# Gate rows, B, first scan tiles, layer norm steps and last tile of a conv and state-space layer moved in the order of work

## The chip, the cores and the metric

The kernel runs on one core of one Trainium2 chip. That core has TensorE (PE) for matrix products, VectorE (DVE), ScalarE (ACT) and GpSimd (POOL) for elementwise work, and SyncE (SP), whose queue issues nearly all DMA transfers. Each engine takes its own instructions strictly in order, and waits where the data or the buffer of the next one is not there yet. The metric is the time of one launch on the device, in microseconds; the median of the runs counts.

## The reference

One layer over 2048 tokens of width 1024, with a context of 256 tokens: a normed and modulated input, one projection to five parts of 1024 columns, a gated depthwise convolution of 31 taps on a 32 x 64 grid with a layer norm behind it, a state-space recurrence in both directions over 64 groups, an output projection with a gate, and a last norm.

```python
h = rmsnorm(x, norm_g) * (1 + scale) + shift
p = split(h @ w_in)                       # value, glu gate, silu gate, u, silu gate of y
# conv branch
v = p[0] * sigmoid(p[1])
v = dwconv_latent(v, conv_dw, conv_db)    # 31 taps: rows of the grid for half the channels, columns for the rest
v = silu(layernorm(v, conv_ln_g, conv_ln_b)) * silu(p[2])
# state-space branch: lam_bar, b_bar from a, log_dt, b; the context gives the first state
hf = scan(u, lam_bar_f, b_bar_f); hb = scan(u, lam_bar_b, b_bar_b, reverse)
y = gelu(real(hf . c_f) + real(hb . c_b) + d * u)
y = y * sigmoid(y @ glu_w + glu_b) * silu(p[4])
mix = concat(v, y) @ w_out
out = rmsnorm(x + gate * mix, final_g)
...
```

## The kernel before

Every large product is split in three: an operand a becomes hi + lo, and hi x hi, lo x hi and hi x lo are summed (lines 129, 134 and 135). `project` makes one 128 x 512 tile of a projection from eight row tiles, that is from 24 such matmuls. `whi` (ACT, line 243) and `wlo` (POOL, line 244) split a weight tile that was loaded as `wraw` (or `wuc`, for the context's columns).

The work goes through five stages, told apart by the line that is busy.

The **head**, to some 163 us, loads x in four blocks of 512 tokens (`xt`), norms and modulates them, and computes the context projections (`psc`, `usc`, stored as `uc_d`) and the first channel tile of the convolution. `gate_rows` adds the output gate's rows into one PSUM tile `gps`; four ACT copies `gr` (line 717) write them to `gate_d`.

The **conv stage**, to some 699 us, takes one channel tile of 128 after the other. PE computes its glu gate and value (`glu`, line 299, writes `v`), and DVE applies the taps of the tile before (`taps`, line 300 on): three accumulators fP, fQ and fR, of which fP and fR lie in PSUM and are begun by ACT (lines 319 and 323) and fQ lies in SBUF; each tap is one DVE instruction of line 336. `beside`, called once behind each projection, emits RATE = 4.8 taps and the glu that is held back, and then takes one step of the generator `toeplitz`. That makes, for four groups at a time, the factors `ff` (POOL products ff and pp, lines 387 and 388, four DVE sums, line 396), the discretised B `bb` (`bbar`, every fourth time), the product `tz` on PE (line 407) and its copy `tzs` to the store `toe_d`. The steps of the generator stand in the code behind the taps of each call, so on DVE the four sums stand behind those taps. The value products go to the pool `mm` with three PSUM banks. At the end, `gate_tiles` begins the projections of the silu gate (`gs`, stored as `cg_d`).

The **scan stage**, to some 1232 us, works in 32 blocks of two groups. `load` fetches U (the inputs), F, M and, for every second block, B. `inputs` builds KB from B and X from KB on POOL (lines 835 to 851), turns X on PE (`et`, line 855), and ACT copies that to E; then come the chunk states S on PE (line 894), the recurrence on DVE and the readout. The tiles B, KB, kt, X, xp, E, ys and the four tt belong to pools of this stage, which open when the conv stage's are closed. The projections of the remaining gate tiles run between them.

The **GLU stage**, to 1417 us, has 32 products of y with `glu_w`. A table `aside` hangs other work behind product n of them; the eight steps of the layer norm of the first 512 tokens (the generator `layer_norm(0)`) are hung behind the products (6, 10, 14, 15, 17, 18, 20, 21). The steps are: loads lx and their sum lsum (POOL); mean mu on PE and squares; variance va and its root, which DVE makes into a diagonal dg; rb, the diagonal spread over a tile on PE, and the multiplies; then four pairs of multiplies by lg, each pair with its own load and stores to `mix_d`.

The **out projection**, from 1417 us on, has sixteen row tiles t_ of four products each. The layer norm of the next 512 tokens runs in four steps behind the products of LN_QUARTER in four row tiles; all four pairs of lg are in the last step and share one buffer. `mix_in` loads `mr` from `mix_d`, and `split_mix` splits it into mh (ACT) and ml (DVE). `finish` norms a row tile and stores it (line 1287).

## Time and profile before

| | us |
|---|---|
| median of three runs (lowest, highest) | 1800.89 (1800.38, 1803.52) |
| the profiled execution, its own time | 1801.97 |
| its span in the profile | 1800.2 |
| PE busy | 1725.8 (96%) |
| weight loads on PE, beside the matmuls | 1354.6 (75%) |
| DVE, ACT, POOL busy | 1410.8 (78%), 584.9 (32%), 561.5 (31%) |

A row of the profile names an engine, a line of the kernel, an operation with its output and inputs (`tz<-ff,bb` is tile tz from ff and bb, buffer numbers left out), how many there were, and in square brackets the idle time of the engine ahead of it with what ended that idle time. PE is busy nearly all the time, so the few places where it is not are what the views are searched for. A busy PE is not PE at its peak: the granted clock says at which of its two levels it ran.

### The profile page before, as it was taken

Reading aid. Unit: us, or ns where it says so; the run is one execution under the profiler, and the core shown is the slowest. Engines: PE = TensorE matmul, PEld = TensorE weight load, DVE = VectorE, ACT = ScalarE, POOL = GpSimd, SP = SyncE. Lnnn points to the kernel's source line nnn. Section 1 sums busy time; section 2 is a strip of 40 time slices with the busy share of each in tenths; the row PEclk is TensorE's granted clock in tenths of the full one; section 3 lists DMA queues with packets and bytes.
Section 4 is the critical chain, followed back from the end, with each engine's and each line's share of the span. In section 5 each row is a group of like instructions: output and inputs, shape, how many; then the busy total and the mean of one; then the engine's idle time right before and its main releaser. Section 6 shows DMA issues by size and latency. Waiting matters only on the chain.

```text
span 1800.2 us, 23670 instructions
## 1 busy us (share of the span) xinstructions
PE 1725.8 (96%) x8728; PEld 1354.6 (75%) x8728; DVE 1410.8 (78%) x2063; ACT 584.9 (32%) x904; POOL 561.5 (31%) x550
## 2 busy tenths in 40 slices
PE   7999799999999998999999999999989989999998
PEld 2675577787788886777777777778778768887887
DVE  7863799999998987999999999995665755656533
ACT  4542211221222113343433433354453422222211
POOL 0632243344432113665554655320210041212000
PEclk9999899999999998999999999999999999999999
DMA  9604131222222123243333333363738837363621
GB/s 342 231 18 127 34 104 44 96 79 68 97 98 76 50 76 109 88 121 106 101 117 115 98 122 105 105 225 120 215 113 279 303 108 206 118 198 122 176 97 44
DMA packets 175724, 227.45 MB, mean 126 GB/s; under 512 B 38516, under 2 KB 117492, under 8 KB 174584
## 3 DMA queue, kind: packets, MB, share of 16 engines
q1 hardware_dynamic: 175608, 225.94, 39.0%
q8 instruction: 69, 1.13, 0.3%
q14 instruction: 47, 0.39, 0.1%
HBM read 147.36 MB, written 78.52 MB: 125 GB/s over the span
## 4 chain that ended last, share of the span: by engine, by line
PE 65%; DVE 20%; DMA 6%; issue 3%; ACT 2%; POOL 2%; SPq 1%; DVEq 0%; ACTq 0%; POOLq 0%
PE ps L129 13%; PE ps L134 13%; PE ps L135 13%; PE pso L135 4%; PE pso L134 4%; PE pso L129 4%; DVE fQ L336 4%; PE S L894 3%; DVE fR L336 3%; PE Y L945 3%; DVE fP L336 3%; DMA mix_d<-lx 2%; PE Y L936 1%; DVE lo L223 1%; PE adps L620 1%
## 5 line engine op out<-in xcount | busy, mean ns | idle before, releaser
L129 PE MATMUL ps<-hi,whi 128*128 128x512 f32 x1248 | 499.1, 400 | 1.2 <-ACT v L296 1.2
L134 PE MATMUL ps<-lo,whi 128*128 128x512 f32 x1248 | 492.7, 395 | 0.0
L135 PE MATMUL ps<-hi,wlo 128*128 128x512 f32 x1248 | 491.6, 394 | 0.3 <-POOL wlo L244 0.3
L129 PEld LDWEIGHTS ps<-hi,whi 128*128 128x128 f32 x1248 | 235.9, 189 | 62.1 <-issue 9.3
L135 PEld LDWEIGHTS ps<-hi,wlo 128*128 128x128 f32 x1248 | 236.1, 189 | 55.5 <-issue 3.5
L134 PEld LDWEIGHTS ps<-lo,whi 128*128 128x128 f32 x1248 | 236.2, 189 | 53.4 <-issue 5.2
L129 PE MATMUL pso<-woh,mh 128*128 128x512 f32 (+1 forms) x528 | 206.2, 391 | 0.8 <-ACT woh L1026 0.4
L134 PE MATMUL pso<-wol,mh 128*128 128x512 f32 (+1 forms) x528 | 203.8, 386 | 2.1 <-DVE wol L1029 2.1
L135 PE MATMUL pso<-woh,ml 128*128 128x512 f32 (+1 forms) x528 | 204.4, 387 | 0.7 <-DVE ml L1029 0.5
L244 POOL TENSOR_TENSOR wlo<-wraw,whi 128x1024 fp32r<-128x1024 f32 x37 | 97.3, 2630 | 174.2 <-ACT whi L243 174.2
L336 DVE SCALAR_TENSOR_TENSOR fQ<-v,sml,fQ 128x960 f32<-128x960 f32 (+11 forms) x120 | 149.2, 1243 | 0.0
L336 DVE SCALAR_TENSOR_TENSOR fP<-v,sml,fP 128x960 f32<-128x960 f32 (+10 forms) x112 | 121.0, 1080 | 24.7 <-ACT fP L319 24.7
L336 DVE SCALAR_TENSOR_TENSOR fR<-fS,comb,fR 128x960 f32<-128x960 f32 (+11 forms) x120 | 128.1, 1067 | 0.0
L918 DVE TENSOR_TENSOR_SCAN t<-mag,t 128x287 f32<-128x287 f32 x128 | 122.0, 1011 | 0.0
L134 PEld LDWEIGHTS pso<-wol,mh 128*128 128x128 f32 x528 | 99.8, 189 | 24.7 <-DVE wol L1029 3.1
L129 PEld LDWEIGHTS pso<-woh,mh 128*128 128x128 f32 x528 | 99.8, 189 | 22.9 <-ACT woh L1026 1.4
L135 PEld LDWEIGHTS pso<-woh,ml 128*128 128x128 f32 x528 | 99.7, 189 | 21.7 <-DVE ml L1029 1.5
L243 ACT ACTIVATE whi<-wraw 128x1024 fp32r<-128x1024 f32 x37 | 39.1, 1055 | 212.2 <-PE ps L134 172.9
L129 PE MATMUL ps<-yh,gwh 128*128 128x512 f32 x256 | 100.7, 393 | 0.0
L134 PE MATMUL ps<-yl,gwh 128*128 128x512 f32 x256 | 99.9, 390 | 0.0
L135 PE MATMUL ps<-yh,gwl 128*128 128x512 f32 x256 | 99.9, 390 | 0.0
L1064 POOL TENSOR_TENSOR lsum<-lx 128x512 f32<-128x512 f32 x4 | 5.5, 1362 | 301.7 <-DMA lx<-cv_d 301.7
(295 smaller groups left out, 2804.8 us busy)
## 6 DMA issues: line engine op xcount, KB each, us to landing
wraw<-in_w_in SPq DMA_DIRECT2D x37, 512.0 KB
mr<-mix_d SPq DMA_DIRECT2D x32, 512.0 KB
wa<-in_w_ada SPq DMA_DIRECT2D x32, 256.0 KB
xt<-in_x_t SPq DMA_DIRECT2D x32, 256.0 KB
u_d<-us SPq DMA_DIRECT2D x32, 256.0 KB
f_d<-ff SPq DMA_DIRECT2D x32, 256.0 KB
cv_d<-v SPq DMA_DIRECT2D x8, 1024.0 KB
cg_d<-gs SPq DMA_DIRECT2D x32, 256.0 KB
```

The lines of the kernel that those rows point to most:

```text
L129: i = nc.tensor.matmul(ps, wh, rh, start=first, stop=False)
L134: nc.tensor.matmul(ps, wh, rl, start=False, stop=False)
L135: last[0] = nc.tensor.matmul(ps, wl, rh, start=False, stop=end)
L223: st(lo, xts[k], sh_, hi.bitcast(F32), op0=ADD, op1=SUB)
L243: act(hi, raw, AF.Copy)
L244: pt(lo, raw, hi.bitcast(F32), op=SUB)
L336: yield st(at(acc, lo_ + o, hi_ + o), at(src, lo_ + j, hi_ + j), tap[n](j), at(acc, lo_ + o, hi_ + o), op0=MUL, op1=ADD)
L620: nc.tensor.matmul(adps[32 * c:32 * c + 32], sil[:, k], was[h, k, c], start=(k == 0), stop=(k == KT - 1), skip_group_check=True)
L894: m = nc.tensor.matmul(Sf[h_, o + c0:o + c1], k.E[:, d, i, h_], seq[g][d][:, c0:c1], start=True, stop=True, skip_group_check=True)
L918: nc.vector.tensor_tensor_scan(dst[:, d, 0:L], mag8[:, g0 + d:g0 + d + 1].to_broadcast([P, L]), src[:, d, 0:L], 0.0, op0=MUL, op1=ADD)
L936: m = nc.tensor.matmul(Y[:, g], k.M[:, g], k.U[:, g, NX:NCOL], start=True, stop=False, skip_group_check=True)
L945: m = nc.tensor.matmul(Y[:, g], k.F[h_, i, d], hs, start=False, stop=(i == 1 and d == 1), skip_group_check=True)
```

## The change

The diff does six things.

The PSUM tile `gps` goes to a new pool `gpp` of one bank, which `tz` uses after it (the pool of tz is gone). The copies `gr` are put into a function `gate_out`, called at the first `beside`, and are ordered on ACT behind the fR of the first channel tile.

`bq`, the load of B for `bbar`, has a tile of its own and is issued with the load of cc, and `beside` steps the generator ahead of the taps, not behind them.

In the scan, B, KB, kt and xp lie in the pool `par`, which is open from the start; X and E take turns in the two buffers of `ff`; ys lies in `stage` and tt in a pool of its own.

The layer norm's steps hang behind the products (6, 10, 14, 16, 18, 19, 20, 21), and for the second norm LN_QUARTER is (0, 5, 8, 10).

In the last row tile, xt times fg is formed piece by piece as `gx` behind each product, and the last scaling is done for one half by ACT, with a store on ACT's own queue, and for the other by DVE.

```diff
-LN_QUARTER = (0, 4, 7, 9)
+LN_QUARTER = ((), (0, 5, 8, 10), (0, 4, 7, 9), (0, 4, 7, 9))
...
+    tp = parstack.enter_context(tc.tile_pool(name="toe", bufs=1))
...
+    gpp = tstack2.enter_context(tc.tile_pool(name="gpp", bufs=1, space=PS))
...
-        act(r_, S_, AF.Identity, scale=tap[2](0), bias=db[:, 1, ct:ct + 1])
+        late.fr = act(r_, S_, AF.Identity, scale=tap[2](0), bias=db[:, 1, ct:ct + 1])
...
+    def b_load(q):
+        bq = late.fir.tile([P, 2, 16, GH], F32, tag="bq", name="bq")
+        for i, nm in enumerate(("b_re", "b_im")):
+            nc.sync.dma_start(bq[:, i], ins[nm][:, 16 * q:16 * q + 16, :])
+        return bq
+
+    def bbar(q, bq):
...
-        bq = stage.tile([P, 2, 16, GH], F32, tag="sa", name="bq")
-        for i, nm in enumerate(("b_re", "b_im")):
-            nc.sync.dma_start(bq[:, i], ins[nm][:, g_, :])
...
+            if b4 % 4 == 0:
+                bq = b_load(b4 // 4)
...
-            tz = late.tps.tile([P, 2, P], F32, tag="tz", name="tz")
+            tz = gpp.tile([P, 512], F32, tag="g", name="tz")[:, 0:2 * P].rearrange("p (d q) -> p d q", d=2)
...
-    gps = nps.tile([P, 512], F32, tag="gps", bufs=1, name="gps")
+    gps = gpp.tile([P, 512], F32, tag="g", name="gps")
...
-    for i in range(2):
-        for c in range(2):
-            gr = stage.tile([1, 512], F32, tag="sa", name="gr")
-            act(gr, gps[64 * i + 32 * c:64 * i + 32 * c + 1], AF.Copy)
-            nc.sync.dma_start(gate_d[i:i + 1, c * 512:(c + 1) * 512], gr)
+
+    def gate_out():
+        for i in range(2):
+            for c in range(2):
+                gr = stage.tile([1, 512], F32, tag="sa", name="gr")
+                g_ = act(gr, gps[64 * i + 32 * c:64 * i + 32 * c + 1], AF.Copy)
+
+                tc.add_manual_dep(g_.ins, late.fr.ins.name, mybir.DependencyInfo(
+                    mybir.DependencyClass.NoSync, mybir.DependencyReason.DATA), reason="order")
+                nc.sync.dma_start(gate_d[i:i + 1, c * 512:(c + 1) * 512], gr)
+
...
         def beside():
 
+            next(toe, None)
             due[0] += RATE
...
-            next(toe, None)
+            if late.fr is not None and not late.gated:
+                late.gated = True
+                gate_out()
...
-                B_ = [s1p.tile([P, 4, GH], F32, tag=f"B{i}", name=f"B{i}") for i in range(2)]
+                B_ = [par.tile([P, 4, GH], F32, tag=f"B{i}", name=f"B{i}") for i in range(2)]
...
-                KB = KBs[b // 2] = [s2p.tile([P, 4, GH], F32, tag=f"KB{i}", name=f"KB{i}") for i in range(2)]
-                kt = s1p.tile([P, 4, GH], F32, tag="kt", name="kt")
+                KB = KBs[b // 2] = [par.tile([P, 4, GH], F32, tag=f"KB{i}", bufs=2, name=f"KB{i}") for i in range(2)]
+                kt = par.tile([P, 4, GH], F32, tag="kt", name="kt")
...
-            X = [s1p.tile(shp, F32, tag=f"X{i}", name=f"X{i}") for i in range(2)]
-            xp = s1p.tile(shp, F32, tag="xp", name="xp")
+            X = tp.tile([P, 2, G, T, GH], F32, tag="ff", bufs=2, name="X")
+            X = [X[:, i] for i in range(2)]
+            xp = par.tile(shp, F32, tag="xp", name="xp")
...
-            k.E = s1p.tile([P, G, 2, P], F32, tag="E", name="E")
+            k.E = tp.tile([P, G, 2, P], F32, tag="ff", bufs=2, name="E")
...
-            tt = k.tt = [s1p.tile([P, G, NCOL], F32, tag=f"t{i}", name=f"t{i}") for i in range(4)]
+            tt = k.tt = [s0p.tile([P, G, NCOL], F32, tag=f"t{i}", name=f"t{i}") for i in range(4)]
...
-            ys = s1p.tile([P, G, NC_], F32, tag="ys", name="ys")
+            ys = stage.tile([P, G, NC_], F32, tag="sa", name="ys")
...
-    for n in (6, 10, 14, 15, 17, 18, 20, 21):
+    for n in (6, 10, 14, 16, 18, 19, 20, 21):
...
-            for cs_ in [slice(0, 1024)] if t_ < 15 else [slice(0, 512), slice(512, 1024)]:
-                st(xt[:, cs_], xt[:, cs_], rs, fg[:, cs_], op0=MUL, op1=MUL)
-                nc.sync.dma_start(ov[row(t_)[0], row(t_)[1], cs_], xt[:, cs_])
+            if t_ < 15:
+                st(xt, xt, rs, fg, op0=MUL, op1=MUL)
+                nc.sync.dma_start(ov[row(t_)[0], row(t_)[1], :], xt)
+                return
+
+            act(xt[:, 0:512], late.gx[:, 0:512], AF.Identity, scale=rs)
+            vs(xt[:, 512:1024], late.gx[:, 512:1024], rs, None, op0=MUL)
+            nc.scalar.dma_start(ov[row(t_)[0], row(t_)[1], 0:512], xt[:, 0:512])
+            nc.sync.dma_start(ov[row(t_)[0], row(t_)[1], 512:1024], xt[:, 512:1024])
...
-                        if t_ < 12 and 4 * (t_ % 4) + 2 * (1 - k8) + i in LN_QUARTER:
+                        if t_ < 12 and 4 * (t_ % 4) + 2 * (1 - k8) + i in LN_QUARTER[t_ // 4 + 1]:
...
+                    if i == 0:
+                        late.gx = wp.tile([P, 1024], F32, tag="wraw", bufs=1, name="gx")
+                    vt(late.gx[:, cols[i]], xt[:, cols[i]], fg[:, cols[i]], op=MUL)
```

On ACT, at the end of the head, this stands in a row before (whi splits a weight tile, v is the glu gate's sigmoid, us a tile of u):

```order
L320 ACTIVATE fQ<-v,sml 128x32x32
L243 ACTIVATE whi<-wraw 128x1024
L428 ACTIVATE us<-ps 128x2x256
L296 ACTIVATE v<-ps 128x512 x2
L717 ACTIVATE gr<-gps 1x512 x4
L319 ACTIVATE fP<-v,db,sml 128x1024
L323 ACTIVATE fR<-fS,db,comb 128x1024
```

and this after:

```order
L321 ACTIVATE fP<-v,db,sml 128x1024
L322 ACTIVATE fQ<-v,sml 128x32x32
L325 ACTIVATE fR<-fS,db,comb 128x1024
L245 ACTIVATE whi<-wraw 128x1024
L435 ACTIVATE us<-ps 128x2x256
L298 ACTIVATE v<-ps 128x512 x2
L726 ACTIVATE gr<-gps 1x512 x4
```

The beginnings fP and fR of the first channel tile moved ahead of the four copies gr, of a weight split and of two v.

On DVE, in the conv stage, around the second set of four sums ff, before:

```order
L336 SCALAR_TENSOR_TENSOR fR<-fS,comb,fR 128x32x27
L336 SCALAR_TENSOR_TENSOR fP<-v,sml,fP 128x32x27
L336 SCALAR_TENSOR_TENSOR fQ<-v,sml,fQ 128x32x28
L299 TENSOR_TENSOR v<-ps,v 128x512
L336 SCALAR_TENSOR_TENSOR fR<-fS,comb,fR 128x32x27
L336 SCALAR_TENSOR_TENSOR fP<-v,sml,fP 128x32x26
L336 SCALAR_TENSOR_TENSOR fQ<-v,sml,fQ 128x32x26
L396 TENSOR_TENSOR ff<-ff,pp 128x256 x4
```

and after:

```order
L338 SCALAR_TENSOR_TENSOR fR<-fS,comb,fR 128x32x27
L403 TENSOR_TENSOR ff<-ff,pp 128x256 x4
L338 SCALAR_TENSOR_TENSOR fP<-v,sml,fP 128x32x27
L338 SCALAR_TENSOR_TENSOR fQ<-v,sml,fQ 128x32x28
L301 TENSOR_TENSOR v<-ps,v 128x512
L338 SCALAR_TENSOR_TENSOR fR<-fS,comb,fR 128x32x27
L338 SCALAR_TENSOR_TENSOR fP<-v,sml,fP 128x32x26
L338 SCALAR_TENSOR_TENSOR fQ<-v,sml,fQ 128x32x26
```

The sums moved ahead of five taps and one glu.

On POOL, in the head, among the splits wlo of the context's weight tiles, before:

```order
L244 TENSOR_TENSOR wlo<-wuc,whi 128x1024 x8
L194 TENSOR_TENSOR sqa<-sqa,sq 128x512
L244 TENSOR_TENSOR wlo<-wuc,whi 128x1024
L194 TENSOR_TENSOR sqa<-sqa,sq 128x512
L244 TENSOR_TENSOR wlo<-wuc,whi 128x1024
```

and after:

```order
L246 TENSOR_TENSOR wlo<-wuc,whi 128x1024 x3
L853 TENSOR_TENSOR KB_5425<-B_5416,kbr 128x64
L856 TENSOR_TENSOR KB_5426<-B_5416,kbi 128x64
L854 TENSOR_TENSOR kt<-B_5417,kbi 128x64
L855 TENSOR_TENSOR KB_5425<-KB_5425,kt 128x64
L857 TENSOR_TENSOR kt<-B_5417,kbr 128x64
L858 TENSOR_TENSOR KB_5426<-KB_5426,kt 128x64
L866 TENSOR_TENSOR xp<-KB_5426,lim 128x256
L246 TENSOR_TENSOR wlo<-wuc,whi 128x1024
L853 TENSOR_TENSOR KB_5605<-B_5560,kbr 128x64
L856 TENSOR_TENSOR KB_5606<-B_5560,kbi 128x64
L854 TENSOR_TENSOR kt<-B_5561,kbi 128x64
```

The products KB and kt of the scan's first two pairs of blocks, and the first xp, moved from the start of the scan to behind the third and the fourth wlo.

## Rows read from the trace of the kernel before

**Rows 1.** The page, part 1: busy time, share of the span, instructions.

```profile
PE 1725.8 (96%) x8728; PEld 1354.6 (75%) x8728; DVE 1410.8 (78%) x2063; ACT 584.9 (32%) x904; POOL 561.5 (31%) x550
```

**Rows 2.** Waits of PE over the span: total us, times, longest.

```profile
PE tz L407 <- DVE ff L396: 21.6, 10, 12.7
...
PE mu L1069 <- POOL lsum L1066: 6.4, 2, 5.6
PE rb L1101 <- DVE dg L171: 5.4, 1, 5.4
```

**Rows 3.** Windows, PE: stretch, length, busy (instructions), granted clock, DMA share, GB/s.

```profile
209.90:214.70 4.80, 4.78 (x38) 0.50 0.34 113
214.70:219.50 4.80, 4.80 (x22) 1.00 0.06 14
262.48:265.90 3.42, 3.42 (x10) 0.50 0.89 278
...
1327.44:1330.85 3.41, 3.18 (x12) 0.50 0.36 108
1453.73:1460.56 6.83, 6.15 (x13) 0.50 0.26 88
```

**Rows 4.** Windows, DVE, in the conv stage: the same columns.

```profile
225.00:540.00 315.00, 313.96 (x352) 0.98 0.24 84
...
571.00:650.00 79.00, 62.66 (x61) 1.00 0.20 74
```

**Rows 5.** Timeline of DVE: start, duration, line, operation, count, [idle before <-releaser].

```profile
191.02 1.26 DVE L336 SCALAR_TENSOR_TENSOR fP<-v,sml,fP 128x992 f32<-128x992 f32 x1 [24.65 <-ACT fP L319]
...
223.30 1.05 DVE L299 TENSOR_TENSOR v<-ps,v 128x512 f32<-128x512 f32 x1
```

**Rows 6.** Timeline of ACT at the end of the head.

```profile
187.46 2.44 ACT L717 ACTIVATE gr<-gps 1x512 f32<-1x512 f32 x4 [1.28 <-PE gps L701]
```

**Rows 7.** Timeline of PE: last matmul of tile 1's first value product.

```profile
218.81 0.39 PE L135 MATMUL ps<-hi,wlo 128*128 128x512 f32 x1
```

**Rows 8.** Taps of line 336, 225 to 540: ns min/median/max, first and last start.

```profile
L336 DVE SCALAR_TENSOR_TENSOR fQ<-v,sml,fQ x74: 800/1180/2919, 225.3 to 537.7; 128x896 f32<-128x896 f32 x11, 128x832 f32<-128x832 f32 x11, 128x960 f32<-128x960 f32 x10, 128x864 f32<-128x864 f32 x8
...
L336 DVE SCALAR_TENSOR_TENSOR fP<-v,sml,fP x69: 802/1114/1256, 224.3 to 536.8; 128x832 f32<-128x832 f32 x12, 128x960 f32<-128x960 f32 x10, 128x896 f32<-128x896 f32 x10, 128x864 f32<-128x864 f32 x8
```

**Rows 9.** Timeline of POOL: a wlo of the head, the scan's first KB.

```profile
67.14 2.70 POOL L244 TENSOR_TENSOR wlo<-wuc,whi 128x1024 fp32r<-128x1024 f32 x1 [0.79 <-ACT whi L243]
...
699.34 0.45 POOL L835 TENSOR_TENSOR KB<-B,kbr 128x64 f32<-128x64 f32 x1 [7.71 <-DMA B<-in_b_re]
```

**Rows 10.** Timeline of DVE: six lo in the head; the last products.

```profile
83.54 12.44 DVE L223 SCALAR_TENSOR_TENSOR lo<-xt,ada,hi 128x512 fp32r<-128x512 f32 x6
...
1795.58 1.42 DVE L1287 SCALAR_TENSOR_TENSOR ox<-ox,orsy,fg 128x512 f32<-128x512 f32 x2
```

**Rows 11.** Timeline of PE at the start of the scan.

```profile
705.53 0.47 PE L855 MATMUL et<-cst,X 128*128 128x128 f32 x1 [6.41 <-POOL X L848]
...
708.61 4.18 PE L894 MATMUL S<-U,E 128*64 128x288 f32 x24 [0.69 <-ACT E L861]
```

**Rows 12.** Timeline of SP there: start and length of an issue.

```profile
695.43 0.42 SPq L809 DMA_DIRECT2D B<-in_b_re  x1
...
701.68 0.58 SPq L804 DMA_DIRECT2D U<-uc_d  x1
```

**Rows 13.** Timelines of SP, DVE and PE around the fifth row tile.

```profile
1523.46 0.80 SPq L1023 DMA_DIRECT2D mr<-mix_d  x2
...
1530.99 1.23 DVE L1029 TENSOR_TENSOR ml<-mr,mh 128x1024 fp32r<-128x1024 f32 x1 [8.85 <-ACT mh L1026]
...
1532.27 0.50 PE L135 MATMUL pso<-woh,ml 128*128 128x512 f32 x1
```

**Rows 14.** Timelines of POOL and DVE: the longest tap, and POOL's work beside it.

```profile
288.32 2.41 POOL L244 TENSOR_TENSOR wlo<-wraw,whi 128x1024 fp32r<-128x1024 f32 x1
...
288.73 2.92 DVE L336 SCALAR_TENSOR_TENSOR fQ<-v,sml,fQ 128x864 f32<-128x864 f32 x1
```

13 lines of the change are left out of this document (7 added, 6 removed).

## The prediction

> **What bounds the kernel now.** The page's first part comes first: PE is busy 1725.8 of 1800.2 us [rows 1], so the order of PE's instructions sets the time, and a change pays only where it shortens one of PE's waits or the low clock behind one. The view of PE's waits names them [rows 2]: the Toeplitz products tz wait 21.6 us for the sums ff on DVE, in ten places, the longest 12.7; mu waits 6.4 for lsum, 5.6 of it in one place; rb waits 5.4 for dg. Then the windows, for the clock [rows 3]: behind the first tz wait PE runs 4.80 us at 0.50 of full speed, which is 1.2 GHz; the next 4.80 us, at 2.4 GHz, hold 22 matmuls, so 0.22 us each and twice that at the low level. The same 0.50 stands in 3.42 us behind a later tz wait (there are three such stretches), in 3.41 behind rb and in 6.83 around mu. Low clock filled with work so costs a little under half its length: 2.2 us behind the first tz wait, 1.6 for each 3.4 us, 3.2 around mu. Last comes DVE in the conv stage: busy 313.96 of 315 us from 225 to 540, but 62.66 of 79 from 571 to 650 [rows 4]. While PE waits for tz, DVE is the bound behind it, and towards the end of the stage it has some 16 us of slack.
>
> **Gate rows and B, small matrices (the conv stage).** DVE stands still for 24.65 us until 191.02, for the first fP on ACT [rows 5]; ACT's copies gr, 2.44 us from 187.46, are just ahead of that fP, and they waited for gps on PE [rows 6]. The change gives gps a bank of its own and puts fP and fR ahead of gr, so the first tap can start as soon as v is there, near 167: DVE begins its uninterrupted work about 24 us earlier. Not all of it is kept, since DVE's queue holds the glu of the value products between the taps. The first of tile 1 starts at 223.30 [rows 5], 4.1 us behind the end of its last matmul on PE, near 219.2 [rows 7], and up to there PE moves only by the first wait, 12.73 idle and 2.2 of clock. So DVE can be 15.0 + 4.1, about 19.2 us, earlier from there on. The moved call of the generator adds to this for tz alone: its four sums stand five taps earlier in DVE's queue, at about 1.1 us each [rows 8], so tz is ready 19.2 + 5.4 = 24.6 us earlier. What PE can get back at most is 21.6 + 2.2 + 3 x 1.6 = 28.6, less about 1 in waits too short to name: 27.6. DVE is the smaller bound, and its slack from 571 to 650 takes up the difference between its 19.2 and PE's 24.6 before the stage ends. I take **-24.6**, between -15.0 (only the first wait goes; then glu holds PE through the three ps banks) and -27.6. The gr copies and gate_d now run beside products and cost nothing: the first tz, which needs their bank, stands ten us of products behind them; without that cover they would cost 2.44.
>
> **What moves into the head.** KB and its loads B no longer wait for a buffer of the scan, and the scheduler puts the first two pairs among the context products: eleven small POOL products and an xp at 0.3 to 0.6 us (the first KB took 0.45 [rows 9]), some 6 us in all, between the wlo products for which PE's context projections wait. The second pair's B loads wait on SP until POOL has read the first pair's, and hold the next x loads about 3 us. The cost lies between 0 and 6, all of it on the path. DVE feels POOL there as well: six lo took 12.44 us from 83.54 [rows 10] beside a full POOL, over 2 us each, where wider taps take 1.1. I take **+2**, the part of the second pair that stands ahead of the wlo at 67.14, which has 0.79 us of slack [rows 9].
>
> **The scan's start.** PE waits 6.41 for X, and S starts at 708.61 [rows 11]. After the change X of the first block is computed in the conv stage, and et follows the last gate tile at once. What is late next is U: its loads stay on SP behind cv_d and behind the second cg_d, which waits for gs of the last gate tile. The last piece of the first block issues at 701.68 [rows 12], without the two B loads near 700.7; the B load issued at 695.43 beside cv_d was landed when POOL started KB at 699.34 [rows 9, 12], 3 to 3.9 us later, so U is there between 703.2 and 704.6. S starts near 703.7 in place of 708.61, and et is no longer split in two by a wait, 0.6 more; the low clock stays, as PE still idles some 4 us. **-5.5**, between -3 and -8. X and E taking two slots in turn is the same limit as one slot each; ys in another pool and tt in its own wait for nothing new.
>
> **Layer norm steps.** In the GLU stage rb moves one projection back, 24 matmuls at 0.23, 5.5 us: its wait of 5.4 is covered, and 1.6 of clock go: **-7.0**, between -5.4 and -7.0. The last step stays after product 21, so the stores that the out projection reads are no later. In the out projection mu of the second norm moves one product back; its 5.6 wait and 3.2 of clock go, 8.8 together. But nothing in its chain gets shorter. lsum sets when mu starts, at the same moment as today; rb, the multiplies, four serial lg loads in one buffer, the mix_d stores, mr and ml follow. Today they end just in time: mr issues at 1523.46, ml runs from 1530.99 for 1.23, and the first matmul that reads it, at 1532.27, waits 0.3 us for it [rows 13]. rb comes about 3 us earlier for want of the low clock, so ml is ready near 1529.2, while PE arrives at 1532.0 - 8.8 = 1523.2. It waits 6.0 there and pays 1.6 of clock again. Net **-1.2**, between +1 and -8.8.
>
> **Last tile.** Two final products take 1.42 us from 1795.58 [rows 10], one behind the other, each with its store. Now ACT and DVE do a half each at once: **-0.7**, between 0 and -1.4. The product gx fits where DVE waits for ACT's square.
>
> **Rule against row.** The fQ taps from 225 to 540 reach 2919 ns at a median of 1180, the fP taps beside them never exceed 1256 [rows 8]; the longest fQ, at 288.73, began inside a wlo of POOL and ended 0.9 us behind it [rows 14]. So POOL stops some taps and not others. The Trainium skill, page "SBUF — State Buffer", section "SBUF: two separate sides", says that an instruction of DVE with two SBUF inputs and one of GpSimd that reads SBUF exclude each other for the whole instruction. By that rule, as an estimate, the four us of X that move beside the taps and all six of KB would be paid, and the time would be 1772. The trace agrees for fQ and disagrees for fP.
>
> **The sum.** -24.6 + 2.0 - 5.5 - 7.0 - 1.2 - 0.7 = -37.0. The profiled execution took 1801.97 (span 1800.2), which gives 1765.0; the median of the runs shown is 1.1 lower, 1800.89, so I forecast **1764**.
>
> **Rivals.**
> (a) The chain of the second norm has more slack than I see and the 8.8 are kept: 1764 - 7.6 = 1756. For it: one lx load less stands on SP ahead of the third lg. Against: the 0.3 us of slack.
> (b) The glu products hold PE: with DVE only 19.2 earlier and the sums ahead of some glu, PE waits for a free ps bank and keeps the first wait alone, 15.0 in place of 24.6: 1774. For it: DVE's 313.96 of 315. Against: today's waits there are of tz and none of ps.
> (c) The scan's start does not do what it says: U lands as late as X did, nothing is gained there, and the head pays 4: 1764 + 5.5 + 2 = 1772.
> (d) Slower: POOL blocks DVE. I count sixteen fQ taps over 1.3 us today, some 15 us above a usual tap in sum, so 0.95 each. In DVE's new phase against POOL all 74 fQ taps from 225 to 540 might meet a POOL instruction: 70 us, 55 more than today, on the engine that bounds the stage: 1819. It decides against the change from 37 us on, that is when about 39 more taps are caught. For it: the 2919 ns. Against: the order of POOL's instructions beside the taps hardly changes.
>
> **How the numbers follow.** Forecast 0.59 (own range 1757 to 1771), (a) 0.13, (b) 0.13, (c) 0.08, (d) 0.04; other ways to no gain 0.03. The range 1752 to 1778 takes in (a) to (c) with a few us of the bounds around them. Faster by over 0.2%, about what a measurement of this kernel can tell from no change, 0.94; within it 0.02; slower 0.04.
>
> **What would show it.** Right: DVE's first taps near 167, no tz wait over 3 us, a wait ahead of S under 5 us, no wait of rb in the GLU stage, and a new wait of some 6 us on ml at the fifth row tile of the out projection. Wrong: ps products waiting for DVE's v in the conv stage (b), a higher median of fQ (d), psc or ps waiting over 2 us more for wlo in the head, S waiting for U past 706 of today's time (c).

## The result, and the profile after

The median of four runs after is 1780.91 us (1780.43 to 1782.68), against 1801.59 for the kernel before on the same chip (four runs, 1800.38 to 1803.52). The ratio is 0.9886, 95% interval 0.9869 to 0.9903: 20.7 us faster. The forecast was 1764, 37 us faster, with a range from 1752 to 1778. The direction was right, the size was not: 17 us are missing, and the time lies outside the range.

The span of the profiled execution fell from 1800.2 to 1779.2. Its page, part 1 (busy time, share, instructions), answers to [rows 1]:

```profile
PE 1725.2 (97%) x8728; PEld 1356.8 (76%) x8728; DVE 1417.6 (80%) x2065; ACT 585.0 (33%) x905; POOL 559.9 (31%) x550
```

PE's busy time is the same within 0.6 us, so the whole gain is idle time. The waits of PE after (total us, times, longest), which answer to [rows 2]:

```profile
PE ps L130 <- DVE v L301: 10.4, 6, 3.7
...
PE rb L215 <- DVE dg L173: 6.8, 1, 6.8
PE pso L135 <- DVE wol L1048: 2.8, 5, 0.8
PE S L913 <- DVE sn L892: 2.5, 1, 2.5
...
PE tz L414 <- DVE ff L403: 1.6, 2, 1.5
```

The waits for tz went from 21.6 us to 1.6. In their place stands a wait of the glu's products ps for v, 10.4 us in six places; before, no such wait is in the list. The rb at line 215 is not the layer norm's (that one, at line 1120, waits no more) but one of the head, where the norm of x is spread: 6.8 us, where it had 1.3 before:

```profile
77.07 1.16 PE L213 MATMUL rb<-dg,cst 128*128 128x128 f32 x8 [1.29 <-DVE dg L171]
```

The first row tile of the out projection waits 2.8 us for wol, in five small pieces.

Where PE's own timeline passes the same instruction in both kernels, the stretches compare as follows (us; the forecast is that of the sum). PE "reaches" an instruction when it is through with the one ahead, which is taken as 0.23 us, a matmul's step at the high level, behind that one's start.

| stretch on PE | before | after | difference | forecast |
|---|---|---|---|---|
| start to where PE reaches the first tz (head and first projections) | 197.0 | 202.5 | +5.5 | +2.0 |
| from there to where it reaches et (conv stage) | 501.9 | 491.2 | -10.7 | -24.6 |
| et to the first projection in the scan | 14.3 | 10.1 | -4.2 | -5.5 |
| to the first product of the GLU stage | 518.8 | 518.1 | -0.8 | 0 |
| GLU stage | 185.1 | 178.2 | -6.9 | -7.0 |
| first row tile of the out projection | 25.9 | 31.5 | +5.5 | 0 |
| second to fourth row tile | 77.4 | 68.6 | -8.7 | -1.2 |
| all behind | 279.7 | 278.9 | -0.7 | -0.7 |
| span | 1800.2 | 1779.2 | -21.0 | -37.0 |

Two terms hold (GLU stage, and nearly the scan's start). Four do not: the conv stage brought less than half, the head cost more, a new loss of 5.5 us stands in the first row tile, and the second norm kept what the forecast had given back.

**The conv stage.** The timeline of DVE after, where its first taps start (start, duration, idle before and releaser in brackets), answers to [rows 5]:

```profile
171.90 1.26 DVE L338 SCALAR_TENSOR_TENSOR fP<-v,sml,fP 128x992 f32<-128x992 f32 x1
...
175.38 2.40 DVE L368 TENSOR_TENSOR bb<-bq,br 128x256 f32<-128x256 f32 x1
195.90 0.43 DVE L369 TENSOR_TENSOR tb<-bq,bi 128x256 f32<-128x256 f32 x1 [18.12 <-ACT gr L726]
```

and the timeline of ACT there, to [rows 6]:

```profile
170.66 1.21 ACT L321 ACTIVATE fP<-v,db,sml 128x1024 f32<-128x1024 f32 x1 [7.19 <-DVE v L301]
...
192.92 2.44 ACT L726 ACTIVATE gr<-gps 1x512 f32<-1x512 f32 x4 [1.24 <-PE gps L708]
```

The first tap starts at 171.90 in place of 191.02, as the change meant. But after three taps and one product of bbar DVE stands still for 18.12 us, and its releaser is gr. The tile tb, a scratch of bbar, has the tag "sa" of the pool `stage`, which has three buffers, and so have the four copies gr. Those wait for gps on PE, which is no earlier than it was. Before, gr was ahead of the taps on ACT and held DVE there; after, it holds DVE through a buffer. In the window from 160 to 205 us (length, busy of DVE, instructions, clock) DVE is busy for 17.20 us of 45:

```profile
160.00:205.00 45.00, 17.20 (x21) 1.00 0.26 81
```

**The head.** Timelines of POOL, DVE and PE after, where the wlo of the context's weights meet the root for rb (lines 64 to 70, on 4 elements a partition):

```profile
72.34 2.39 POOL L246 TENSOR_TENSOR wlo<-wuc,whi 128x1024 fp32r<-128x1024 f32 x1 [2.34 <-ACT whi L245]
...
74.94 2.44 POOL L246 TENSOR_TENSOR wlo<-wuc,whi 128x1024 fp32r<-128x1024 f32 x1
...
78.79 2.57 POOL L246 TENSOR_TENSOR wlo<-wuc,whi 128x1024 fp32r<-128x1024 f32 x1 [0.18 <-ACT whi L245]
81.32 2.60 POOL L196 TENSOR_TENSOR sqa<-sqa,sq 128x512 f32<-128x512 f32 x2
```

```profile
72.25 0.16 DVE L69 TENSOR_TENSOR nrxp<-nrxp,nv 128x4 f32<-128x4 f32 x1
72.44 2.31 DVE L70 SCALAR_TENSOR_TENSOR nrxy<-nrxp,nrxy 128x4 f32<-128x4 f32 x1
...
75.03 2.35 DVE L69 TENSOR_TENSOR nrxp<-nrxp,nv 128x4 f32<-128x4 f32 x1
...
79.07 2.30 DVE L70 SCALAR_TENSOR_TENSOR nrxy<-nrxp,nrxy 128x4 f32<-128x4 f32 x1
81.41 1.19 DVE L68 SCALAR_TENSOR_TENSOR nrxp<-nrxy 128x4 f32<-128x4 f32 x1
```

```profile
84.72 2.08 PE L215 MATMUL rb<-dg,cst 128*128 128x128 f32 x8 [6.80 <-DVE dg L173]
```

A root step takes 0.16 us alone, and 2.3 us when it meets a wlo on POOL, that is as long as the wlo. Three meetings cost 6.5 us on the path to rb; two more, with the sums sqa of 1.3 us each, make steps of 1.19 and 1.11. PE stands for 6.80, and the window around it is at 1.2 GHz (columns as above, the clock is the 0.50):

```profile
83.10:89.90 6.80, 5.18 (x24) 0.50 0.01 2
```

**The out projection.** The windows of PE after (length, busy, clock, DMA share, GB/s) over the first row tile, and the longest of its waits in PE's timeline:

```profile
1407.70:1417.70 10.00, 8.46 (x35) 1.00 0.95 293
1417.70:1428.00 10.30, 8.81 (x20) 0.50 1.02 383
```

```profile
1417.20 0.50 PE L135 MATMUL pso<-wol,mh 128*128 128x512 f32 x1 [0.76 <-DVE wol L1048]
```

PE reaches this tile 17.1 us earlier than before, but the last split wol in it starts only 13.7 us earlier (on DVE at 1422.17, where it stood at 1435.82). The loads of `w_out` run beside it at 293 to 383 GB/s. No wait is over 0.76 us, but from 1417.7 to 1428.0 the clock is at 1.2 GHz: the tile's four products take 31.5 us, where at the high level and without waits four products take 22.0 (the thirteenth to fifteenth row tile). The waits for wol and woh are 3.6 us in sum. Before, they were 2.5 us, in four pieces of up to 0.77, and the clock did not fall beside them:

```profile
1431.00:1443.20 12.20, 9.63 (x38) 1.00 1.04 379
```

So of the 5.5 us some 1.1 are longer waits, and the rest is the low clock.

The second norm went the other way. PE's rows for mu and for the first product that reads ml in the fifth row tile, which answer to the third line of [rows 2] and to [rows 13]:

```profile
1442.59 1.02 PE L1088 MATMUL mu<-lsum,cst 128*128 128x512 f32 x2
...
1512.54 0.50 PE L136 MATMUL pso<-woh,ml 128*128 128x512 f32 x1 [0.53 <-DVE ml L1048]
```

mu waits no more, and ml, forecast to cost 6.0, costs 0.53.

**The scan's start** on PE after, which answers to [rows 11]:

```profile
693.73 0.60 PE L874 MATMUL et<-cst,X 128*128 128x128 f32 x4
696.82 0.67 PE L913 MATMUL S<-U,E 128*64 128x288 f32 x2 [2.49 <-DVE sn L892]
699.06 4.08 PE L913 MATMUL S<-U,E 128*64 128x288 f32 x22 [1.57 <-DMA U<-uc_d]
```

et follows at once, as forecast; S then waits 2.49 and 1.57 us.

**The end.** Timelines of ACT and DVE for the two halves, and the packets of the two stores (queue, kind: packets, MB, share) from 1776.0 to 1776.8 us and from 1777.05 to 1777.8:

```profile
1774.86 0.72 ACT L1310 ACTIVATE ox<-gx,orsy 128x512 f32<-128x512 f32 x1 [2.58 <-issue]
```

```profile
1774.82 0.49 DVE L1311 TENSOR_SCALAR ox<-gx,orsy 128x512 f32<-128x512 f32 x1
```

```profile
q1 hardware_dynamic: 117, 0.24, 79.8%
```

```profile
q10 hardware_dynamic: 107, 0.19, 66.2%
```

From PE's last matmul to the end it is 8.4 us, 8.7 before: 0.3 saved. The two halves are scaled side by side, but their stores move one behind the other: the packets of SP's queue run from 1776.16 to 1777.01, those of ACT's from 1776.83 to 1777.69. Together they take 1.5 us, as the two stores on one queue did before (1797.20 to 1798.71). What is saved lies ahead of the first packet.

### The profile page after: what moved, and what is told of

Read it like the earlier page. It is cut to its first block, busy times and chain, and to the rows that moved or that the text cites. A ratio compares the mean times of both kernels' runs of the same rounds, so it can differ in the third digit from the quotient of the medians.

```text
span 1779.2 us, 23678 instructions
## 1 busy us (share of the span) xinstructions
PE 1725.2 (97%) x8728; PEld 1356.8 (76%) x8728; DVE 1417.6 (80%) x2065; ACT 585.0 (33%) x905; POOL 559.9 (31%) x550
## 5 line engine op out<-in xcount | busy, mean ns | idle before, releaser
L130 PE MATMUL ps<-hi,whi 128*128 128x512 f32 x1248 | 500.1, 401 | 11.6 <-DVE v L301 10.4
L130 PEld LDWEIGHTS ps<-hi,whi 128*128 128x128 f32 x1248 | 236.1, 189 | 75.4 <-DVE v L301 12.8
```

The costliest lines, as they stand in the source:

```text
L130: i = nc.tensor.matmul(ps, wh, rh, start=first, stop=False)
```

## The experiments

Four things were in question: the conv stage (tb's buffer, the moved call), the head (the scan's products on POOL or its loads on SP), the layer norm's tables, and the low clock of the first row tile. The kernel before was run beside each of four groups of them, with medians of 1801.52, 1802.35, 1802.93 and 1803.34 us, so a difference under 2 us between kernels of different groups says little. The labels e2 and e3 in the expectations are those of two kernels, named below where they come.

**tb in a buffer of its own** (on the kernel after).

```diff
-        tb = stage.tile(shp, F32, tag="sa", name="tb")
+        tb = late.fir.tile(shp, F32, tag="tb", name="tb")
```

> The changed kernel, with tb (the scratch tile of the small matrices B) in a buffer of its own, not in the pool that the four gr copies use. Theory A: in the changed kernel DVE starts three taps at 171.9 us and then stands 18.1 us for tb, whose buffer a gr copy holds; that is why the conv stage gained only about 10 us of the 24.6 forecast. Without it DVE has no gap over 2 us before 200, PE's waits of ps products for v (10.4 us) and the low clock behind them go, and the time is 1766 to 1771. Rival B: the three ps banks and DVE's load bound the stage anyway; the gap is refilled by waits for v further on, and the time is 1777 to 1781.

Measured: 1769.0 us (1767.91 to 1769.51), ratio 0.9814 (0.9798 to 0.983), 11.9 less than after. DVE's timeline and its window show the standstill gone:

```profile
177.62 0.41 DVE L369 TENSOR_TENSOR tb<-bq,bi 128x256 f32<-128x256 f32 x1
```

```profile
160.00:205.00 45.00, 28.45 (x31) 1.00 0.29 92
```

The conv stage takes 482.7 us, 19.2 less than before and 8.5 less than after. So tb's buffer was the cause of 8.5 of the 13.9 us that are missing in this stage; the other 3 us come behind it, most of all in the first row tile (1.8) and the GLU stage (1.0). The head is as slow as in the kernel after (202.5). The waits for v, which theory A had going, stay for the most part:

```profile
PE ps L130 <- DVE v L301: 8.2, 4, 3.0
```

**B and KB of the scan out of the head** (e2; on the kernel after; `late.cc` is the last load of cc, `late.pp` the last product pp, and the two dependences only order the instructions on SP and on POOL).

```diff
-                    nc.sync.dma_start(t_, ins[nm][:, G * b:G * b + 4, :])
+                    i = nc.sync.dma_start(t_, ins[nm][:, G * b:G * b + 4, :])
+                    if b == 0:
+                        tc.add_manual_dep(i.ins, late.cc.ins.name, mybir.DependencyInfo(
+                            mybir.DependencyClass.NoSync, mybir.DependencyReason.DATA), reason="order")
...
-                pt(KB[0], B_[0], a, op=MUL)
+                i = pt(KB[0], B_[0], a, op=MUL)
+                if b == 0:
+                    tc.add_manual_dep(i.ins, late.pp.ins.name, mybir.DependencyInfo(
+                        mybir.DependencyClass.NoSync, mybir.DependencyReason.DATA), reason="order")
```

> The changed kernel, with the first B load ordered on SP, and the first KB product on POOL, behind the last load and product of the Toeplitz generator, so that none of them runs in the head; the first X is still made in the conv stage. Theory A: the KB products and the later wlo of the head run against DVE's small root steps (2.3 us each in place of 0.2), which makes rb of the head wait 6.8 us where it waited 1.3, with 6.8 us of low clock behind it; without them the first tz is reached 5.5 us earlier. Since the stage behind is bound by DVE, whose 18.1 us wait is tied to PE's gps, all 5.5 us come through: 1774 to 1777. Rival: the wait in the head has another cause (the order of SP's loads of x and weights), and the time stays at 1780 to 1782.

Measured: 1768.61 us (1766.91 to 1770.15), ratio 0.9811 (0.9791 to 0.9831), 12.3 less than after, more than the head's own share and below what either theory had. PE reaches the first tz at 195.5, 7.0 earlier than after. The rest comes later: the conv stage is 2.9 shorter (its mean granted clock is 1.00 in place of 0.98, while the waits for v grow from 10.4 to 12.3), and the scan's start, the first row tile and the last ones give 0.7, 1.0 and 0.7.

**Both together** (e3, "the kernel with both repairs" below). The two diffs above.

> The changed kernel with both edits, tb in its own buffer and nothing of KB in the head. Theory A: the two add up, 13 and 5.5 us: 1761 to 1766. Rival: once DVE starts early, the glu places bound PE (as forecast for the rival of the glu products), and one of the two is lost: 1768 to 1775.

Measured: 1761.33 us (1759.31 to 1763.36), ratio 0.9772 (0.9753 to 0.9791). The gains don't add (19.6 less than after, where the two are 24.2): the conv stage takes 482.4, as with tb alone. What is left is the wait for v; tz is not in the list of waits:

```profile
PE ps L130 <- DVE v L301: 7.9, 4, 3.0
```

So with the head and tb mended the conv stage stands against DVE by way of the glu, as rival (b) said, though at -19.5 and not at the -15 that (b) had.

**The layer norm's tables alone** (on the kernel before).

```diff
-LN_QUARTER = (0, 4, 7, 9)
+LN_QUARTER = ((), (0, 5, 8, 10), (0, 4, 7, 9), (0, 4, 7, 9))
...
-    for n in (6, 10, 14, 15, 17, 18, 20, 21):
+    for n in (6, 10, 14, 16, 18, 19, 20, 21):
```

> The kernel before, with the two tables of layer norm steps alone changed. In the changed kernel rb's wait of 5.4 and mu's of 5.6 are gone, no wait of 6 us on ml stands at the fifth row tile (0.5 only), but PE runs 10.2 us at low clock around the waits for wol at the first row tile, which cost 5.5 us. Theory A: all three belong to the tables: 7 + 9 - 5.5, so 1790 to 1792, with the low clock at the first row tile. Rival 1: the low clock there belongs to another part: 1784 to 1787. Rival 2, the forecast: the second norm gives back all but 1.2: 1792 to 1795, with a wait on ml.

Measured: 1790.55 us (1787.63 to 1794.81), ratio 0.9936 (0.9913 to 0.9959). In the profiled execution the GLU stage takes 178.3 in place of 185.1, and the first four row tiles 97.3 in place of 103.3; ml is not waited for. The first row tile is longer here too, 28.6 in place of 25.9, with 6.8 us of low clock in it. The tables alone bring 11 us, where the forecast had 7.0 + 1.2. The runs spread over 7 us; which of the row tiles varies was not seen, as one of them only is profiled.

**Fourteen products without their loads** (on the kernel with B and KB out of the head): products of the same sizes, whose result is not read, stand on POOL behind the wlo where the KB products stood.

```diff
+                for j in range({2: 7, 3: 5, 4: 1, 6: 1}.get(ct, 0)):
+                    n = 256 if ct == 2 and j == 6 else 64
+                    i = pt(late.dm[:, 0:n], sml[:, 0:n], sml[:, 64:64 + n], op=MUL)
...
```

> The kernel of e2 (no KB and no B load in the head), with fourteen products on POOL that nobody reads, of the same sizes and at the same places behind the third to the seventh wlo where the changed kernel had its KB products; SP's queue in the head is that of e2. Theory: POOL's instructions alone shift the wlo behind them onto DVE's root steps, so rb of the second block waits 5 to 7 us again and low clock follows: 1774 to 1781, as the changed kernel. Rival: the B loads on SP, which wait for POOL and hold x and the weights, are the cause: the wait stays 1.3 us and the time 1767 to 1770.

Measured: 1770.73 us (1769.21 to 1773.43), ratio 0.9832 (0.981 to 0.9855): 2.1 more than without them, inside the intervals. The wait for rb is 1.4 us. POOL's timeline:

```profile
71.41 2.44 POOL L246 TENSOR_TENSOR wlo<-wuc,whi 128x1024 fp32r<-128x1024 f32 x1 [0.49 <-ACT whi L245]
...
78.56 2.53 POOL L246 TENSOR_TENSOR wlo<-wuc,whi 128x1024 fp32r<-128x1024 f32 x1 [3.98 <-ACT whi L245]
```

The wlo starts at 71.41 and the next one at 78.56, and between them the root's multiplies run undisturbed. PE reaches the first tz at 197.0. The kernels of this section that have neither the products nor the loads in the head reach it between 195.5 and 198.1, so the products' own time, which the forecast had priced at 2, can't be told from nothing here; it does not make the 6.8 us.

**Loads without most products** (on the kernel with tb alone): the second part of the diff for B and KB without the first, so that only the KB product that is written first is ordered behind pp, and the B loads are not. Two of the products stay in the head with the first pair's loads.

> The kernel after with bbar's scratch tb in a buffer of its own, as in the run that did that alone, and with the first KB product ordered behind the last pp on POOL; the loads of the first B tiles stay early on SP, in the head. So the head has the loads but not the fourteen products. The kernel with tb alone (both early) took 1769.0 and that with neither early 1761.33. Theory that the loads on SP are what costs in the head, since the weight loads wuc stand behind the second pairs' B loads: with the products late, the B buffers come free late too, so the second pair's B loads move behind them and only the first pair's two loads stay in the head; then 1761 to 1763, and rb in the head waits under 2 us. Rival, that the first loads on SP in front of x and the weights are enough: 1766 to 1769 and rb waits some 6 us.

Measured: 1762.53 us (1759.89 to 1771.62), ratio 0.9784 (0.9755 to 0.9813). The profiled execution is the one of 1771.62, and the other three took 1759.89 to 1762.9, so the median is that of the theory and the profile that of the rival. In the profiled one rb waits 6.7 us:

```profile
85.17 2.08 PE L215 MATMUL rb<-dg,cst 128*128 128x128 f32 x8 [6.72 <-DVE dg L173]
```

**Loads alone.** As the last, with all the first pair's products ordered behind pp, so that only two B loads stand in the head.

```diff
-                pt(kt, B_[1], c, op=MUL)
+                i = pt(kt, B_[1], c, op=MUL)
+                if b == 0:
+                    tc.add_manual_dep(i.ins, late.pp.ins.name, mybir.DependencyInfo(
+                        mybir.DependencyClass.NoSync, mybir.DependencyReason.DATA), reason="order")
...
-                pt(KB[1], B_[0], c, op=MUL)
+                i = pt(KB[1], B_[0], c, op=MUL)
...
```

> The run before had two of the fourteen products in the head beside the first pair's loads. Here every KB and kt product is ordered behind the last pp, so that of the whole scan only the first pair's two B loads stand in the head; tb has its own buffer. Compared with the kernel that has neither in the head (1761.33), the two loads change what the scheduler put behind them: on ACT the split whi of a weight tile stands behind two more hi. Theory that this order is the cause, since it brings that whi, and so a wlo of 2.4 us on POOL, some 2 us later onto DVE's small root steps: rb in the head waits over 5 us, and the total is 1767 to 1770, or some executions near it where the two meet and others near 1760 where they don't. Rival, that POOL's products (two of them at least) are needed: rb waits under 2 us and 1760 to 1763 in all executions.

Measured: 1766.72 us (1760.09 to 1769.86), ratio 0.9805 (0.978 to 0.9831); the profiled execution is the one of 1760.09. Here the four are 1760.1, 1766.0, 1767.4 and 1769.9. POOL, DVE and PE in the profiled one:

```profile
72.68 4.74 POOL L246 TENSOR_TENSOR wlo<-wuc,whi 128x1024 fp32r<-128x1024 f32 x2 [3.06 <-PE psc L136]
...
80.60 2.41 POOL L246 TENSOR_TENSOR wlo<-wuc,whi 128x1024 fp32r<-128x1024 f32 x1 [1.93 <-ACT whi L245]
```

```profile
72.79 2.28 DVE L70 SCALAR_TENSOR_TENSOR nrxy<-nrxp,nrxy 128x4 f32<-128x4 f32 x1
75.11 2.34 DVE L68 SCALAR_TENSOR_TENSOR nrxp<-nrxy 128x4 f32<-128x4 f32 x1
```

```profile
80.79 1.16 PE L215 MATMUL rb<-dg,cst 128*128 128x128 f32 x8 [1.07 <-DVE dg L173]
```

Two wlo meet the root; the third starts at 80.60, when the root is through, and rb waits 1.07. The two meetings alone cost nothing that shows: PE reaches the first tz at 196.3, among the 195.5 to 198.1 above. In the profiled execution of the run ahead of this one the third started at 79.31 and met it. Between these two executions, of kernels that differ by two small products, PE is 6.8 us apart where it reaches the first tz (203.1 and 196.3), and 11.5 at the end of the span.

What the two loads change is the order that the scheduler writes. ACT's timeline here, and in the kernel with both repairs:

```profile
70.93 0.73 ACT L224 ACTIVATE hi<-xt,ada 128x512 fp32r<-128x512 f32 x1 [1.53 <-DVE lo L225]
71.56 1.04 ACT L245 ACTIVATE whi<-wuc 128x1024 fp32r<-128x1024 f32 x1
```

```profile
69.55 1.06 ACT L245 ACTIVATE whi<-wuc 128x1024 fp32r<-128x1024 f32 x1 [0.19 <-issue]
```

With the loads the whi stands behind one more hi, which waits for a lo of DVE, and it comes 2 us later. In the kernel with both repairs its wlo runs from 70.69 to 73.1, meets a lo of DVE, and POOL then idles to 77.7 while the root's multiplies run (74.3 to 76.6). With the loads the wlo begins at 72.68 and the next one follows at once, on the root. So the loads, by the order, bring the splits onto the root. Whether a third one meets it is decided by 1.3 us in its start (80.60 and 79.31); where it does, PE reaches the first tz 6.8 us later. The times of the executions without a profile (three between 1759.9 and 1762.9 in the run ahead, three between 1766.0 and 1769.9 here) fit two such cases; that they come from this place is not shown.

**The splits of w_out, two behind each product** (on the kernel with both repairs): the table of `w_split` evened out.

```diff
-    for n, todo in ((24, (0, 1)), (25, (2,)), (26, (3, 4)), (27, (5, 6)), (28, (7,)), (29, (8,)), (30, (9, 10)),
-                    (31, (11, 12, 13, 14, 15))):
+    for n, todo in ((24, (0, 1)), (25, (2, 3)), (26, (4, 5)), (27, (6, 7)), (28, (8, 9)), (29, (10, 11)), (30, (12, 13)),
+                    (31, (14, 15))):
```

> The kernel of e3, with the splits of the output weights spread evenly over the last eight products of the GLU stage, two behind each, where five stood behind the last one. In e3 the first row tile of the out projection takes 30.9 us for four products that take 22.0 at full clock: waits for woh and wol of some 3 us and low clock. Theory: these waits come from the five splits behind the last product, and the layer norm's table makes PE come there earlier; without them 6 to 9 us go: 1752 to 1756. Rival: the weight loads bound the splits, the waits stay or move into the GLU stage: 1758 to 1763.

Measured: 1759.62 us (1759.11 to 1761.01), ratio 0.977 (0.9746 to 0.9795): 1.7 less than with both repairs, inside the intervals. The first row tile takes 27.8 us in place of 30.9. Its low clock falls from 10.2 us to 3.4, its waits do not fall (3.1 us in sum, one of 1.7 for woh; 2.8 with both repairs).

**The splits earlier still** (on the same kernel): three behind products 24 and 25, two behind 26 to 29, one behind 30 and 31.

```diff
-    for n, todo in ((24, (0, 1)), (25, (2,)), (26, (3, 4)), (27, (5, 6)), (28, (7,)), (29, (8,)), (30, (9, 10)),
-                    (31, (11, 12, 13, 14, 15))):
+    for n, todo in ((24, (0, 1, 2)), (25, (3, 4, 5)), (26, (6, 7)), (27, (8, 9)), (28, (10, 11)), (29, (12, 13)), (30, (14,)),
+                    (31, (15,))):
```

> The kernel with tb in its own buffer and B and KB behind the conv stage's Toeplitz products (1761.33), with the splits of w_out in the GLU stage hung earlier: three behind products 24 and 25, two behind 26 to 29, one behind 30 and 31, where the table has 2, 1, 2, 2, 1, 1, 2 and 5, and the run with two behind each took 1759.62. Theory that the low clock of the first row tile (its four products take 30.9 us, and 27.8 in the run with two each, where 22.0 is full clock) comes from waits on woh and wol alone: no wait on them, the row tile at 22 to 24 us, total 1754 to 1757. Rival, that other waits of the row tile (mh, ml, or the products' first loads) hold it, or that the early splits stand in the way of the GLU stage's own work on DVE and ACT: the row tile stays at 27 or more, or the GLU stage grows beyond 178.3; total 1759 to 1763.

Measured: 1756.3 us (1754.76 to 1757.72), ratio 0.9742 (0.9725 to 0.9759). It is the fastest kernel of the study, 45 to 47 us under before and 5.0 under the kernel with both repairs; the intervals of the two touch, their runs do not overlap. One wait is left in the first row tile, and the clock is whole:

```profile
PE pso L135 <- DVE wol L1054: 0.8, 1, 0.8
```

```profile
1390.00:1400.00 10.00, 9.44 (x41) 1.00 0.89 302
1400.00:1406.30 6.30, 6.11 (x27) 1.00 1.09 330
```

The row tile takes 23.2 us, near the 22.0 of full clock, and the GLU stage grows by 0.5. So the late splits are the cause of the tile's loss, by waits for woh and wol under 0.8 us and the low clock that stands beside them. The waits do not bring the low clock every time: in the last run of this section (the generator's step behind the taps) the same tile has six such waits, 3.2 us in sum, and stays at the high level; it takes 26.9:

```profile
1400.00:1414.80 14.80, 11.58 (x45) 1.00 1.03 381
```

What decides it is not shown. So of the 7.7 us that the tile gains between the two profiled executions, some 4 came to that other kernel without earlier splits.

**mu back in its place** (on the kernel with both repairs).

```diff
-LN_QUARTER = ((), (0, 5, 8, 10), (0, 4, 7, 9), (0, 4, 7, 9))
+LN_QUARTER = ((), (0, 4, 7, 9), (0, 4, 7, 9), (0, 4, 7, 9))
```

> The kernel of e3, with the second norm's steps at their old places, (0, 4, 7, 9). Theory: the chain behind rb has slack when rb comes one product later, so that moving mu saved its 5.6 us of wait and some low clock in full: 1767 to 1771 here, with a wait of 5 us or more of mu. Rival, the forecast: the chain gives back all but 1.2 us: 1761 to 1764.

Measured: 1769.43 us (1766.38 to 1772.18), ratio 0.9823 (0.9799 to 0.9847): 8.1 more. The wait is back, with low clock behind it:

```profile
PE mu L1094 <- POOL lsum L1091: 3.8, 1, 3.8
```

Of the 8.1, the profiled execution shows 6.6 in the second to fourth row tile (75.4 in place of 68.8). So the step is worth nearly all of its wait and clock, and nothing gives it back at ml. It is not the longer first row tile that makes room for it: with the earliest splits, where that tile takes 23.2, the second to fourth take 68.6 as well.

**The generator's step behind the taps again** (on the kernel with both repairs).

```diff
-            next(toe, None)
             due[0] += RATE
...
+            next(toe, None)
             if late.fr is not None and not late.gated:
```

> The kernel of e3, with the generator's step again behind the taps of each call, as in the kernel before; everything else as in e3, where PE waits nowhere for ff and 7.9 us for v in the conv stage, with two stretches of low clock. The forecast took 19.2 us for DVE's earlier start and 5.4 for the moved step. Theory: without the move the four sums come 5 to 6 us later in DVE's queue and PE waits for tz in several places, 4 to 6 us and their low clock, while the waits for v shrink: 1763 to 1769. Rival: DVE's load alone sets the stage's length, waits for v turn into waits for tz one for one: 1760 to 1763.

Measured: 1762.75 us (1760.69 to 1766.8), ratio 0.9789 (0.9765 to 0.9813): 1.4 more, inside the intervals. The waits change their name:

```profile
PE tz L414 <- DVE ff L403: 8.3, 10, 2.6
```

v is not waited for, tz is. The conv stage takes 484.4 in place of 482.4, and the three other kernels with the same conv stage (the two with other splits, the one with mu back) took 480.1, 480.9 and 483.9. So the moved call is worth some 2 us, between 0.5 and 4.3, and hardly clear of that spread.

## Why the prediction was wrong, step by step

**What bounds the kernel** was right: PE is as busy as before, and the 21 us are waits and low clock.

**Conv stage, -24.6 forecast, -10.7 measured: the step that failed.** It is the sentence "DVE begins its uninterrupted work about 24 us earlier". The first tap did start 19 us earlier (the head took 5 of the 24), but the work was interrupted: the forecast priced gps's bank and ACT's order, and did not follow gr's own buffer, the tag "sa", to the next who uses it. tb is in that tag, the line stands in `bbar`. With tb mended the stage gives -19.2, so the buffer is 8.5 of the 13.9 that are missing; the other 5.4 are the next point.

That -19.2 is also DVE's figure of the forecast, 15.0 + 4.1, is in part luck. The forecast put the glu of tile 1 19.2 us earlier in the stage. It was 26.3 us behind where PE reaches the first tz before (223.30 and 197.0), and with tb mended it is 9.9 behind (212.37 and 202.5), 16.4 earlier: its lag of 4.1 us behind PE's matmul did not go, it is 3.0.

```profile
212.37 1.07 DVE L301 TENSOR_TENSOR v<-ps,v 128x512 f32<-128x512 f32 x1
```

**The 5.4 us for the moved call** was a second mistake, in the same term. The call puts the sums, and every fourth time the six products of bbar, ahead of five taps and a glu: tz comes earlier, but that glu's v later. DVE is busy 314 of 315 us from 225 to 540 in either order, so PE waits for it at the one or at the other. The run with the call behind the taps turns the one wait into the other and differs by some 2 us; with DVE's earlier start alone its stage gives -17.5, where the forecast had 19.2. The forecast had assumed that the slack from 571 to 650 takes up the difference; that was too late for the early part of the stage, where the glu waits (from 285 to 480 with both repairs). Rival (b), with chance 0.13, named this mechanism; with tb and the head mended it leaves -19.5, where (b) had -15.

**Head, +2 forecast, +5.5 measured.** The forecast counted twelve products of POOL, fourteen stood there, and their own time, priced at 2, can't be told from nothing (197.0 at the first tz, among 195.5 to 198.1 without them). The row not looked for was the queue's order behind the B loads, and what POOL's wlo lands on: the forecast had seen that six lo took twice their time beside POOL [rows 10], but not that instructions of 4 elements take 2.3 us there, and that eleven such instructions, the root, lie on the path to rb.

**Scan's start, -5.5 forecast, -4.2 measured.** Right in kind: et at once, then a wait for U. Between them stands a wait for sn on DVE, which was not named. With both repairs the stretch is 9.4 us, -4.9.

**GLU stage, -7.0 forecast, -6.9 measured.** Right, by the wait and the clock as written.

**Second norm, -1.2 forecast, -8.7 measured.** The step "nothing in its chain gets shorter" failed, and rival (a) was right. From the start of rb to the end of ml it took 45.6 us before (1486.66 to 1532.22) and 40.6 after (1471.85 to 1512.48). The parts are: rb to the last pair of multiplies by lg 2.9 shorter, from there to the issue of mr 1.1, and from there to ml 0.9. What shortens each was not tried; that mr, mh and ml of the earlier row tiles stand elsewhere between these steps is a guess from the timelines.

**First row tile, not in the forecast, +5.5.** A gain upstream of a chain that does not move as far: some 1.1 us of longer waits, and low clock, which such waits bring in some kernels and not in others. The forecast looked for the chain behind the moved step (ml) and not for the one behind the whole stage: w_out's loads and splits, which were just in time (three short waits for wol and one for woh there before).

**Last tile, -0.7 forecast, -0.3 measured.** The forecast took both final products for the path. Before, the second of them (0.71) ran beside the issue of the first half's store, and behind the first packet the two stores take 1.5 us in either kernel.

**Rival (d)** did not come: the fQ taps from 225 to 540 have a median of 1156 ns and a longest of 2990, as before.

**Rule against row.** The forecast said of the page "SBUF — State Buffer", section "SBUF: two separate sides", of the Trainium skill that the trace disagrees for fP. That was misread: fP and fR lie in PSUM, so their taps have one SBUF input, and the rule, which speaks of DVE instructions with two, does not speak of them. The trace agrees for fQ, and for the head's root steps: those with two inputs in SBUF took 2.3 us beside a wlo and 0.16 alone. By the rule the sum was estimated at 1772, with four us of X and all six of KB paid. The runs show no cost of KB's products that is clear of the spread, and fQ taps beside X as before; it is the wlo, brought to another place, that holds DVE.

**In sum**: of the 16.0 us that are missing in the span, 13.9 are the conv stage, 3.5 the head, 5.5 the first row tile, 1.3 the scan's start and 0.4 the end; 7.5 came back at the second norm, and some 1 in small pieces. The range was too narrow at its upper end, for a reason that can be said: each rival moved one term by a wait that the trace showed, and none was a buffer shared with something that the change had just made later. Of the signs of being right, the first taps (171.90), tz, S and rb came; the wait on ml did not. Of the signs of being wrong, one came, the products ps waiting for v (b).

**What stays open**: what brings the low clock beside waits under a microsecond; which executions of the kernels with B loads in the head have the third meeting (all four of the kernel after lie within 2.3 us, and its profiled one has it); what varies in the runs with the tables alone; and the three parts by which the second norm's chain got shorter.

## What to carry to other kernels

When a wait is taken from one engine, list every buffer that the late instruction writes, and who takes that buffer next; here four copies of 512 numbers cost 8.5 of a 19.2 us gain through a scratch tile of the same tag. After a gain, go to the next stage and ask which loads and splits were just in time there: a row of waits under a microsecond can cost several by the clock, though not every time, and hanging the splits a few products earlier was worth 5 us. And when a scheduler sets the order, even two loads whose data nobody waits for can move another engine's work onto a chain of tiny instructions.

## What the runs showed of the hardware

- DVE instructions on 4 elements a partition, 0.15 to 0.16 us alone, took 2.28 to 2.35 us when they met a 2.4 us wlo on POOL, and 1.11 to 1.21 when they met a 1.3 us sum sqa; all of these have two inputs in SBUF (line 68 reads one tile twice). For the path, their size says nothing; the length of what POOL runs beside them does.
- TensorE fell to 1.2 GHz, from 1417.7 to 1428.0 us, with no wait over 0.76 us anywhere near: ahead of it stood four waits for woh and wol of 0.18 to 0.76 us within 12 us. The same waits do not always do it: with the generator's step behind the taps six of 0.16 to 0.76 us stand within 6 us (1402.7 to 1408.7), and in the kernel before four of 0.41 to 0.77 within 6 us, and both stay at 2.4 GHz. With one such wait left, in the run with the earliest splits, it stayed at 2.4 GHz through the whole row tile.
- Two stores of 256 KB on two queues, issued 0.3 us apart, moved one behind the other, 0.85 us each, and took the same 1.5 us together as on one queue.
